# A gated hybrid block on one core: the opening's loads in written order, and side loads placed by unit

## The chip, the core and the metric

The kernel runs on one core of one Trainium2 chip. The metric is the time of one execution on the device, in microseconds (us). Times are taken as the median of several runs; one further execution is recorded by the hardware profiler, and its profile and trace are what is read here.

## What is computed

One sub-layer for a sequence of 1024 rows of width 2048, everything in float32:

```python
mod = c_act @ w_ada + b_ada                       # 3 x 2048
shift, scale, gate = split(mod, 3)
h = rms_norm(x, g_pre) * (1 + scale) + shift      # 1024 x 2048
q_a, f_a, i_a, z_a, gate_bb, gate_cc, v_b, z_b = split(h @ w_in, 8)   # w_in 2048 x 8192
y_a = rms_norm(hgrn2_chunkwise(q_a, log_f, k_a, i_a), g_head_a) * silu(z_a)
y_b = gate_bb * conv3(gate_cc * v_b) * silu(z_b)
m_a, m_b = split(sigmoid(h @ w_merge + b_merge), 2)                   # w_merge 2048 x 4096
out = (m_a * (y_a @ w_up_a) + m_b * (y_b @ w_up_b)) @ w_o
return x + gate * rms_norm(out, g_post)
```

## The kernel before

Each large product is a two by two block product done with seven products in place of eight (Strassen's way; the stages are called p1, p6, p2, p7, p5, p4, p3), on sums and differences of the blocks. To keep float32's precision, each operand is split into a high part in a rounded format (`w_hi`) and the rest (`w_lo`), and each product is three matmuls: high by high, high by low, low by high. `mm3` (L118) issues them, L119, L122 and L123 being the three. `split_w` (L126) makes a weight tile's high part on ScalarE and its low part on VectorE (L131); `split_h` (L134) does it for the other operand, its low part on VectorE at L136.

**Opening.** `load_x` (L177) loads x as 16 tiles of 512 KB, `norm_x` scales the rows, `transpose_x` turns them with TensorE into 16 tiles `xT`, copied out of PSUM by VectorE and ScalarE in turn (L209 to 212). `ada_pair(q)`, for q = 0 to 3, makes a quarter of scale and shift from 16 tiles of w_ada (`ada_load`, L218, 512 KB each): the scale row with one-row matmuls on TensorE (`prow`, L235), the shift row with sums on VectorE (`row_v`, L237 and L239). Small matmuls then turn both rows into columns. `factors_a` applies them to `xT` and makes the operands of the first four stages, `fp1`, `fp6`, `fp2` and `fp7`, of a pair of groups g; eight groups in all. The tiles of x, xT, w_ada and the factors share 38 buffers of 512 KB (tag "big"); every third w_ada tile goes into one of four buffers of its own (tag "ada").

**Units.** `unit_a(u)` (L328) runs 48 times, 32 units for w_in and 16 for w_merge. `load_q` (L323) loads a unit's four 512 KB weight tiles `a11`, `a21`, `a22`, `a12` into five buffers (tag "raw"). VectorE makes the sums s1 and s2 (L338, L339), s4 (L350) and a11 - a21 (L354), and TensorE the products p1, p6, p2 and p7 with the splits of a11, s2, a12 and a11 - a21, 24 matmuls each, into the PSUM tiles `px` and `py`. s1, s4 and the results go to DRAM for the second phase.

**Side work.** The loop over units (L400) also writes, for the units up to 14 that are even, `factors_b(u // 2)` (L287; four sums, L292 to L295, three splits and three stores), which prepares operands for the second phase; for units 16 to 31 two `gate_step`s each (L362), one w_ada tile's load (L365) and two VectorE sums, every eighth followed by a small matmul `pg` (L377); and for the even units from 32 on `sums_o` (L388), four w_o loads and four sums.

**Second phase and after.** The products p5, p4 and p3 of every unit (tile `pz` first), with the recurrence and the convolution beside them; then the two `up` passes, the output projection and the end.

**What sets the order.** The kernel writes instructions unit by unit; the framework's scheduler then orders each engine's queue by its own estimate of times, within the dependences. SP issues all loads in the order of its queue. An instruction given to `keep_in_program_order` keeps its place among the others so given; an instruction written within `issue_after(i)` comes after i.

Of the kernel before, what the change touches and what calls it, by code (L numbers as in the profile page):

```python
# [983 lines left out]
```

## Time and profile before

| | |
|---|---|
| Median of 3 runs | 2768.53 us (2767.21 to 2771.9) |
| The profiled execution's own time | 2769.2 us |
| Its span | 2767.5 us |
| TensorE busy | 2673.0 us, 97% |
| VectorE, ScalarE, GpSimd busy | 62%, 33%, 10% |
| Mean granted TensorE clock | 0.984 of full |

The span goes from the first to the last instruction of the profiled execution; the time adds what lies around it. Busy shares are means over stages that differ. A granted clock of 1.00 is 2.4 GHz, TensorE's upper level; 0.50 would be 1.2 GHz, the lower one.

### The profile page before, as it was taken

To read this page: it belongs to the slowest core of one execution; us is meant where nothing else is said; L and a number is where in the kernel's file an instruction comes from. 1 tells how busy PE (TensorE), PEld (TensorE's weight loads), DVE (VectorE), ACT (ScalarE), POOL (GpSimd) and SP (SyncE) were. 2 spreads that over 40 slices of the span, in tenths; PEclk is the share of its full clock that TensorE was granted. 3 is DMA by queue.
4 is the path that set the end of the run, shared out by engine and by line. 5 is a ranking of instruction groups with operands and counts; after the bars stand their busy time and mean duration, and the time that the engine had idled before them with its cause. 6 is when DMAs were issued, how large, how long until landed. Compare 5 with 4: busy or idle time off the path is not lost.

```text
span 2767.5 us, 31307 instructions
## 1 busy us (share of the span) xinstructions
PE 2673.0 (97%) x11851; PEld 2152.7 (78%) x11851; DVE 1716.7 (62%) x2096; ACT 906.3 (33%) x1176; POOL 280.0 (10%) x495
## 2 busy tenths in 40 slices
PE   4889999999999999999999999999998999999997
PEld 3267878888888888888888888888885787888786
DVE  6777886754554444546666666656563666765667
ACT  4433222222222222233344444435442222232333
POOL 2012111110000000010000000002111101100000
PEclk9899999999999999999999999999998999999999
DMA  9769999985556655584444444359999569773353
GB/s 361 286 201 313 345 349 364 346 292 179 179 192 179 182 175 177 174 316 137 133 130 133 138 146 138 110 178 374 360 363 407 187 213 335 235 282 99 99 178 142
DMA packets 420071, 631.30 MB, mean 228 GB/s; under 512 B 19564, under 2 KB 281808, under 8 KB 419792
## 3 DMA queue, kind: packets, MB, share of 16 engines
q1 hardware_dynamic: 358528, 394.31, 44.7%
q0 software_dynamic: 60208, 230.78, 21.7%
q10 hardware_dynamic: 1184, 4.20, 0.4%
q8 instruction: 93, 1.52, 0.2%
q14 instruction: 58, 0.48, 0.0%
HBM read 431.04 MB, written 198.18 MB: 227 GB/s over the span
## 4 chain that ended last, share of the span: by engine, by line
PE 81%; issue 8%; DMA 7%; DVE 2%; POOL 1%; ACT 1%; DVEq 0%; POOLq 0%; ACTq 0%; SPq 0%
PE po L866 10%; PE pz L119 7%; PE pz L122 7%; PE pz L123 7%; PE px L119 6%; PE px L123 6%; PE px L122 6%; PE py L123 6%; PE py L119 6%; PE py L122 6%; PE pw L119 4%; PE pw L122 4%; PE pw L123 4%; DMA yp<-yf_scr 3%; DMA ga_raw<-in_w_ada_dram 2%
## 5 line engine op out<-in xcount | busy, mean ns | idle before, releaser
L130 ACT CAST w_hi<-w_raw 128x1024 fp32r<-128x1024 f32 (+1 forms) x296 | 290.9, 983 | 1001.6 <-PE px L122 402.5
L131 DVE TENSOR_TENSOR w_lo<-w_raw,w_hi 128x1024 fp32r<-128x1024 f32 (+1 forms) x296 | 335.7, 1134 | 273.1 <-ACT w_hi L130 263.4
L123 PE MATMUL py<-fp,w_lo 128*128 128x512 f32 x768 | 301.2, 392 | 6.9 <-DVE w_lo L131 6.9
L123 PE MATMUL px<-fp,w_lo 128*128 128x512 f32 x768 | 300.9, 392 | 5.2 <-DVE w_lo L131 5.2
L119 PE MATMUL px<-fp,w_hi 128*128 128x512 f32 x768 | 301.2, 392 | 0.0
L122 PE MATMUL py<-fp,w_hi 128*128 128x512 f32 x768 | 299.5, 390 | 1.3 <-DVE fp L136 1.3
L119 PE MATMUL py<-fp,w_hi 128*128 128x512 f32 x768 | 299.8, 390 | 0.9 <-ACT w_hi L130 0.9
L122 PE MATMUL px<-fp,w_hi 128*128 128x512 f32 x768 | 300.0, 391 | 0.0
L866 PE MATMUL po<-w_hi,lt 128*128 128x512 f32 x896 | 244.2, 390 | 0.6 <-DVE og L900 0.6
L866 PEld LDWEIGHTS po<-w_hi,lt 128*128 128x128 f32 x896 | 168.1, 188 | 37.2 <-DVE og L900 2.2
L130 ACT CAST w_hi<-s 128x512 fp32r<-128x512 f32 (+1 forms) x112 | 90.1, 805 | 285.9 <-PE py L122 245.5
L123 PEld LDWEIGHTS py<-fp,w_lo 128*128 128x128 f32 x768 | 144.5, 188 | 41.5 <-DVE w_lo L131 11.2
L123 PEld LDWEIGHTS px<-fp,w_lo 128*128 128x128 f32 x768 | 144.8, 188 | 36.9 <-DVE w_lo L131 6.5
L122 PEld LDWEIGHTS py<-fp,w_hi 128*128 128x128 f32 x768 | 144.5, 188 | 32.1 <-DVE fp L136 1.7
L122 PEld LDWEIGHTS px<-fp,w_hi 128*128 128x128 f32 x768 | 145.1, 189 | 30.8 <-issue 0.5
L119 PEld LDWEIGHTS px<-fp,w_hi 128*128 128x128 f32 x768 | 144.9, 189 | 30.8 <-issue 0.7
L119 PEld LDWEIGHTS py<-fp,w_hi 128*128 128x128 f32 x768 | 144.5, 188 | 30.8 <-ACT w_hi L130 1.3
L119 PE MATMUL pz<-fp,hi 128*128 128x512 f32 x384 | 152.5, 397 | 3.0 <-DVE d L701 3.0
L122 PE MATMUL pw<-fp,w_hi 128*128 128x512 f32 x384 | 150.8, 393 | 0.0
L119 PE MATMUL pz<-fp,w_hi 128*128 128x512 f32 x384 | 150.5, 392 | 0.0
L123 PE MATMUL pz<-fp,lo 128*128 128x512 f32 x384 | 150.4, 392 | 0.0
L119 PE MATMUL pw<-fp,w_hi 128*128 128x512 f32 x384 | 150.4, 392 | 0.0
(286 smaller groups left out, 4959.4 us busy)
## 6 DMA issues: line engine op xcount, KB each, us to landing
w_raw<-in_w_in_dram SPq DMA_DIRECT2D x160, 512.0 KB, 5.2
s_scr<-s POOLq DMA_DIRECT2D x96, 512.0 KB, 6.0
s_raw<-s_scr SPq DMA_DIRECT2D x96, 512.0 KB, 4.3
w_raw<-in_w_merge_dram SPq DMA_DIRECT2D x80, 512.0 KB, 5.7
u_scr<-o POOLq DMA_DIRECT2D x48, 768.0 KB, 7.5
ada_raw<-in_w_ada_dram SPq DMA_DIRECT2D x64, 512.0 KB, 10.8
yf_scr<-yp POOLq DMA_DIRECT2D x56, 512.0 KB, 9.0
yp<-yf_scr SPq DMA_DIRECT2D x56, 512.0 KB, 12.8
```

The source lines that it names most:

```text
L119: mm = nc.tensor.matmul(o, ah, bh, start=first, stop=False, skip_group_check=True)
L122: nc.tensor.matmul(o, ah, bl, start=False, stop=False, skip_group_check=True)
L123: nc.tensor.matmul(o, al, bh, start=False, stop=last, skip_group_check=True)
L130: nc.scalar.copy(out=hi, in_=raw)
L131: nc.vector.tensor_sub(out=lo, in0=raw, in1=hi.bitcast(F32))
L866: nc.tensor.matmul(o, a, b[:, c], start=st, stop=sp, skip_group_check=True)
```

## The change

1. Loads of x, of w_ada, of unit 0's and 1's weights, and the gate's and w_o's, go through `load`, which keeps them in written order.
2. Unit 0's loads, its sums and three of its weight splits are written ahead of `ada_pair(3)` (`unit_a` is now a generator, stopped at `yield`); its products p1, p6 and p2 are pinned in the order groups 0 to 5 of each, then 6 and 7 of each, with p2 in a PSUM tile of its own. All the rest of unit 0 is issued after the last factor of `factors_a`.
3. From unit 2 on, a11 has one buffer of its own; the other three tiles share the five.
4. `factors_b` is written behind units 2, 4, ..., 16 and issued after that unit's last sum. The gate loads are written at units 10 to 25, two a unit, the w_o loads at the even units 26 to 40; their sums are issued after the last sum of the unit that follows.
5. Buffers: the three small row tables share one raw buffer; `row_p` lies in unit 0's result tile `o0`; only the last quarter of w_ada uses a set of its own, every fourth tile, two buffers in place of four.
6. In the second half of `transpose_x`, four of the eight copies on VectorE go to ScalarE.

```diff
-    rows_c = const.tile([16, P], F32, name="rows_c")
+    rows = wp.tile([P, S], F32, tag="raw", name="rows", bufs=5)
+    rows_a, rows_b, rows_c = rows[0:80, 0:P], rows[0:49, P:2 * P], rows[0:16, 2 * P:3 * P]
...
+    def load(o, i):
+        tc.keep_in_program_order(nc.sync.dma_start(out=o, in_=i))
...
+    o0 = ph.tile([P, 3, HS], F32, name="o0", bufs=1)
...
-            nc.sync.dma_start(out=t, in_=x[si * P:(si + 1) * P, q * S:(q + 1) * S])
+            load(t, x[si * P:(si + 1) * P, q * S:(q + 1) * S])
...
-            if k % 2:
+            if k % 2 and (hf == 0 or k % 4 == 1):
                 nc.vector.tensor_copy(out=xT[k][:, halves[hf]], in_=p)
...
-        if n_ada[0] % 3:
+        if q < 3 or n_ada[0] % 4:
             raw = bigt(F32, "ada_raw").rearrange("p (k e) -> p k e", k=2)
         else:
-            raw = ph.tile([P, 2, HS], F32, tag="ada", name="ada_raw", bufs=4)
-        nc.sync.dma_start(out=raw, in_=w_ada_v[:, k:k + 2, t, q * HS:(q + 1) * HS])
+            raw = ph.tile([P, 2, HS], F32, tag="ada", name="ada_raw", bufs=2)
+        load(raw, w_ada_v[:, k:k + 2, t, q * HS:(q + 1) * HS])
...
-        row_p, row_v = (ph.tile([P, HS], F32, tag=t, name=t) for t in ("row_p", "row_v"))
+        row_p, row_v = o0[:, 0], ph.tile([P, HS], F32, tag="row_v", name="row_v")
...
+    def load_a(u):
+        view, e1, e2 = units[u]
+        if u > 1:
+            a11 = ph.tile([P, 8, P], F32, tag="a11", name="a11")
+            nc.sync.dma_start(out=a11, in_=view[:, 0, :, e1:e1 + P])
+        else:
+            a11 = load_q(view, 0, e1, pin=True)
+        return [a11] + [load_q(view, *a, pin=u < 2) for a in ((0, e2), (1, e2), (1, e1))]
...
+    def unit_a(u, raws):
+        a11, a21, a22, a12 = raws
+        o = ph.tile([P, 3, HS], F32, tag="o", name="o", bufs=2) if u else o0
...
+        s4 = ph.tile([P, 8, P], F32, tag="s4", name="s4") if u else s1
...
         if u == 0:
-            for gs in (range(6), (6, 7)):
-                product(px, w1, fa["p1"], pin=True, gs=gs)
-                product(py, w6, fa["p6"], pin=True, gs=gs)
+            v.tensor_sub(out=a21, in0=a11, in1=a21)
+            w2 = split_w(a12, out_t=(ph.tile([P, 8, P], F32R, name="hi3a", bufs=1), wp.tile([P, 8, P], F32R, tag="raw", name="lo3a", bufs=5)))
+            yield
+            p2 = ps("mm", "p2")
+            for gs in (range(6), (6, 7)):
+                for p, w, f in ((px, w1, "p1"), (py, w6, "p6"), (p2, w2, "p2")):
+                    product(p, w, fa[f], pin=True, gs=gs)
...
-        product(px, split_w(a12), fa["p2"], more=True)
-        nc.scalar.copy(out=o[:, 0], in_=px)
-        nc.vector.tensor_sub(out=a21, in0=a11, in1=a21)
+        if u:
+            product(px, split_w(a12), fa["p2"], more=True)
+            nc.scalar.copy(out=o[:, 0], in_=px)
+        else:
+            v.tensor_add(out=o[:, 0], in0=o[:, 2], in1=p2)
+        if u:
+            v.tensor_sub(out=a21, in0=a11, in1=a21)
         product(py, split_w(a21), fa["p7"], more=True)
-        nc.vector.tensor_add(out=o[:, 2], in0=o[:, 2], in1=py)
+        last_sum[0] = v.tensor_add(out=o[:, 2], in0=o[:, 2], in1=py).ins
...
     for q in range(1, 4):
+        if q == 3:
+            first = unit_a(0, load_a(0))
+            next(first)
         ada_pair(q)
         factors_a((2 * q - 2, 2 * q - 1))
-    factors_a((6, 7), vec=(7,))
+    with tc.issue_after(factors_a((6, 7), vec=(7,)).ins):
+        next(first, None)
...
     def gate_step(n):
...
-        nc.sync.dma_start(out=raw, in_=w_ada_v[:, 2 * kq:2 * kq + 2, 2, eb * HS:(eb + 1) * HS])
+        load(raw, w_ada_v[:, 2 * kq:2 * kq + 2, 2, eb * HS:(eb + 1) * HS])
+        yield
...
     def sums_o(g):
...
-            nc.sync.dma_start(out=t, in_=w_o_v[:, par, g, :, c, :])
+            load(t, w_o_v[:, par, g, :, c, :])
+        yield
...
+    side = []
     for u in range(NU):
-        unit_a(u)
-        if u < 16:
-            if u % 2 == 0:
-                factors_b(u // 2)
-        elif u < 32:
-            gate_step(2 * u - 32)
-            gate_step(2 * u - 31)
-        elif u % 2 == 0:
-            sums_o((u - 32) // 2)
+        if u:
+            for _ in unit_a(u, load_a(u)):
+                pass
+
+        with tc.issue_after(last_sum[0]):
+            if u in range(2, 18, 2):
+                factors_b(u // 2 - 1)
+            for f in side:
+                next(f, None)
+        side = []
+        if 10 <= u < 26:
+            side = [gate_step(2 * u - 20), gate_step(2 * u - 19)]
+        elif u in range(26, 42, 2):
+            side = [sums_o((u - 26) // 2)]
+        for f in side:
+            next(f)
```

In the three places that follow, a name's number is its tile's, and tiles are numbered in the order in which they are written.

SP's queue from the last tile of x on; `w_raw` are weight tiles of the units, `ga_raw` the gate's. Before:

```order
L180 DMA x_1_429<-in_x_dram 128x1024
L224 DMA ada_raw<-in_w_ada_dram 128x2x512 x4
L325 DMA w_raw<-in_w_in_dram 128x8x128 x5
L224 DMA ada_raw<-in_w_ada_dram 128x2x512 x60
L325 DMA w_raw<-in_w_in_dram 128x8x128 x21
L365 DMA ga_raw<-in_w_ada_dram 128x2x512
L325 DMA w_raw<-in_w_in_dram 128x8x128
L365 DMA ga_raw<-in_w_ada_dram 128x2x512 x4
```

Now:

```order
L119 DMA x_1_428<-in_x_dram 128x1024
L119 DMA ada_raw<-in_w_ada_dram 128x2x512 x48
L119 DMA w_raw<-in_w_in_dram 128x8x128 x4
L119 DMA ada_raw<-in_w_ada_dram 128x2x512 x16
L119 DMA w_raw<-in_w_in_dram 128x8x128 x4
L318 DMA a_1443<-in_w_in_dram 128x8x128
L311 DMA w_raw<-in_w_in_dram 128x8x128 x7
```

Before, four w_ada tiles and five weight tiles follow x, then the other 60 w_ada tiles, with the weights of the first six units and the gate's first loads behind them. Now 48 w_ada tiles follow x, then unit 0's four weight tiles, the last 16 of w_ada and unit 1's four. Within the 64 w_ada tiles the numbers jump before (the first four are 722, 732, 746 and 756, the 60 begin 714, 716, 724, 730); now they rise in pairs, a scale and a shift tile, as `ada_pair` reads them.

VectorE where unit 0's weight sums stand. Before, between the factors of the last groups (`a_c`, `sh_c`: the columns of scale and shift):

```order
L338 TENSOR_TENSOR s1_1184<-w_raw_1177,w_raw_1179 128x1024
L248 SCALAR_TENSOR_TENSOR a_c_397<-a_c_397,cols_386 128x4
L339 TENSOR_TENSOR s2_1185<-s1_1184,w_raw_1175 128x1024
L354 TENSOR_TENSOR w_raw_1177<-w_raw_1175,w_raw_1177 128x1024
L266 TENSOR_SCALAR xT_14_570<-xT_14_570,a_c_397,sh_c_398 128x1024
L266 TENSOR_SCALAR keep3_1136<-xT_15_577,a_c_397,sh_c_398 128x512
L266 TENSOR_SCALAR xT_15_577<-xT_15_577,a_c_397,sh_c_398 128x512
L350 TENSOR_TENSOR s4_1186<-w_raw_1181,s2_1185 128x1024
L278 TENSOR_TENSOR xT_12_556<-keep3_1136,xT_12_556 128x512
L278 TENSOR_TENSOR xT_14_570<-keep3_1136,xT_14_570 128x512
L131 TENSOR_TENSOR w_lo_1197<-s2_1185,w_hi_1196 128x1024
L136 TENSOR_TENSOR fp1_6_1143<-xT_12_556,fp1_6_1143 128x512
```

Now, between the third and the fourth quarter of the shift row:

```order
L243 SCALAR_TENSOR_TENSOR row_v_904<-ada_raw_963,c_act_379,row_v_904 128x512 x2
L134 TENSOR_TENSOR w_lo_1030<-w_raw_1017,w_hi_1029 128x1024
L251 TENSOR_TENSOR a_c_396<-pa_970,cols_384 128x4
L253 TENSOR_TENSOR sh_c_397<-pa_970,cols_384 128x4
L252 SCALAR_TENSOR_TENSOR a_c_396<-a_c_396,cols_384 128x4
L336 TENSOR_TENSOR s1_1025<-w_raw_1019,w_raw_1021 128x1024
L337 TENSOR_TENSOR s2_1026<-s1_1025,w_raw_1017 128x1024
L341 TENSOR_TENSOR w_raw_1019<-w_raw_1017,w_raw_1019 128x1024
L241 TENSOR_SCALAR row_v_1046<-ada_raw_1049,c_act_379 128x512
L134 TENSOR_TENSOR lo3a_1042<-w_raw_1023,hi3a_1041 128x1024
L243 SCALAR_TENSOR_TENSOR row_v_1046<-ada_raw_1049,c_act_379,row_v_1046 128x512
L134 TENSOR_TENSOR w_lo_1037<-s2_1026,w_hi_1036 128x1024
```

The sums and low parts of unit 0 have moved ahead of the last quarter's sums (`row_v_1046`) and of the factors that hang on it.

VectorE at the first of `factors_b` (the four sums into `xx`). Before, right behind the last factor of the opening:

```order
L131 TENSOR_TENSOR w_lo_1283<-w_raw_1177,w_hi_1282 128x1024
L136 TENSOR_TENSOR fp7_7_1168<-xT_14_570,fp7_7_1168 128x512
L292 TENSOR_TENSOR xx_1312<-fp6_0_886 128x512
L293 TENSOR_TENSOR xx_1312<-fp2_0_894 128x512
L294 TENSOR_TENSOR xx_1312<-xx_1312 128x512
L295 TENSOR_TENSOR xx_1312<-keep0_871,xx_1312 128x512
L131 TENSOR_TENSOR w_lo_1344<-w_raw_1329,w_hi_1343 128x1024
L136 TENSOR_TENSOR fb0_0_1317<-xx_1312,fb0_0_1317 128x512
```

Now, behind unit 2's last sum (`o_1451`), with sums of units 3 and 4 around it:

```order
L360 TENSOR_TENSOR w_raw_1736<-a11_1734,w_raw_1736 128x1024
L362 TENSOR_TENSOR o_1451<-o_1451,py_1456 128x512
L297 TENSOR_TENSOR xx_1580<-fp6_0_883 128x512
L298 TENSOR_TENSOR xx_1580<-fp2_0_891 128x512
L134 TENSOR_TENSOR w_lo_1643<-s2_1607,w_hi_1642 128x1024
L299 TENSOR_TENSOR xx_1580<-xx_1580 128x512
L337 TENSOR_TENSOR s2_1744<-s1_1743,a11_1734 128x1024
L300 TENSOR_TENSOR xx_1580<-keep0_868,xx_1580 128x512
```

Before, all eight of `factors_b` stand within units 0 to 5; now one stands behind every second unit from 2 to 16.

## Rows read from the trace of the kernel before

**Rows 1.** The page, list of engines: busy us (share of the span) xinstructions

```profile
PE 2673.0 (97%) x11851; PEld 2152.7 (78%) x11851; DVE 1716.7 (62%) x2096; ACT 906.3 (33%) x1176; POOL 280.0 (10%) x495
```

**Rows 2.** Windows: us, PE, PEld, DVE, ACT, POOL busy (x), PEclk, DMA share, GB/s

```profile
0.00:20.00 20.00, 3.73 (x14) 2.54 (x14) 10.49 (x27) 11.53 (x19) 10.29 (x17) 1.00 0.91 336
20.00:40.00 20.00, 14.24 (x81) 12.33 (x82) 15.38 (x36) 15.39 (x27) 6.26 (x5) 0.92 1.11 347
40.00:60.00 20.00, 16.50 (x66) 6.27 (x64) 16.23 (x23) 3.17 (x6) 0.00 (x0) 1.00 1.05 387
60.00:80.00 20.00, 7.20 (x21) 3.94 (x22) 4.24 (x6) 0.57 (x1) 0.00 (x0) 0.52 0.89 325
80.00:100.00 20.00, 19.34 (x51) 5.24 (x51) 16.40 (x28) 10.10 (x15) 0.00 (x0) 0.84 0.55 184
100.00:120.00 20.00, 17.65 (x45) 4.12 (x43) 16.62 (x29) 10.10 (x15) 0.00 (x0) 0.87 1.04 383
```

**Rows 3.** Timeline, TensorE: start us, us, engine line op, xcount [idle before]

```profile
136.10 3.38 PE L235 MATMUL prow<-ada_raw,c_act 128*1 128x512 f32 x4 [2.75 <-DMA ada_raw<-in_w_ada_dram]
...
142.04 0.48 PE L119 MATMUL px<-fp,w_hi 128*128 128x512 f32 x1
...
143.01 0.63 PE L119 MATMUL px<-fp,w_hi 128*128 128x512 f32 x1
...
143.44 0.63 PE L122 MATMUL px<-fp,w_hi 128*128 128x512 f32 x1
...
168.79 0.39 PE L119 MATMUL py<-fp,w_hi 128*128 128x512 f32 x1
...
174.23 0.39 PE L119 MATMUL px<-fp,w_hi 128*128 128x512 f32 x1
```

**Rows 4.** Timeline, VectorE, the opening

```profile
73.49 0.48 DVE L237 TENSOR_SCALAR row_v<-ada_raw,c_act 128x512 f32<-128x512 f32 x1 [15.80 <-DMA ada_raw<-in_w_ada_dram]
...
98.08 0.49 DVE L237 TENSOR_SCALAR row_v<-ada_raw,c_act 128x512 f32<-128x512 f32 x1 [3.32 <-DMA ada_raw<-in_w_ada_dram]
...
103.72 1.54 DVE L239 SCALAR_TENSOR_TENSOR row_v<-ada_raw,c_act,row_v 128x512 f32<-128x512 f32 x2 [2.71 <-DMA ada_raw<-in_w_ada_dram]
...
135.11 4.68 DVE L239 SCALAR_TENSOR_TENSOR row_v<-ada_raw,c_act,row_v 128x512 f32<-128x512 f32 x6
...
142.36 1.21 DVE L338 TENSOR_TENSOR s<-w_raw 128x1024 f32<-128x1024 f32 x1
```

**Rows 5.** Waits of TensorE, 142 to 175 us: us, times, longest

```profile
PE py L123 <- DVE w_lo L131: 2.7, 1, 2.7
PE px L123 <- DVE w_lo L131: 2.2, 1, 2.2
PE py L122 <- DVE fp L136: 1.3, 1, 1.3
```

**Rows 6.** Tiles pz and pg: ns min/median/max, first and last start us

```profile
L119 PE MATMUL pz<-fp,w_hi x384: 389/389/499, 1213.6 to 2086.9; 128*128 128x512 f32 x192
...
L377 PE MATMUL pg<-gacc,ones x8: 591/592/592, 301.0 to 393.6; 128*128 128x512 f32 x8
```

**Rows 7.** Windows, units 1 to 47, columns as in rows 2

```profile
200.00:280.00 80.00, 75.46 (x324) 61.37 (x323) 64.54 (x80) 28.08 (x39) 15.58 (x30) 0.98 0.90 314
...
600.00:900.00 300.00, 300.00 (x1325) 248.09 (x1324) 151.33 (x140) 70.94 (x82) 22.93 (x43) 1.00 0.59 184
...
sum 1039.40, PE 1031.25 PEld 848.18 DVE 617.67 ACT 256.19 POOL 121.96; mean PE 171.88 PEld 141.36 DVE 102.94 ACT 42.70 POOL 20.33
```

**Rows 8.** Factors_b's first sum, gate loads, SP's waits, landing of weights

```profile
L292 DVE TENSOR_TENSOR xx<-fp x8: 679/686/693, 164.8 to 253.1; 128x512 f32<-128x512 f32 x8
...
L365 SPq DMA_DIRECT2D ga_raw<-in_w_ada_dram x32: 367/394/4886, 263.4 to 377.4; - x32
...
SPq L365 <- DVE gacc L374: 25.3, 19, 3.2
...
w_raw<-in_w_in_dram SPq DMA_DIRECT2D x160, 512.0 KB, 5.2
```

More of the change, by code (lines that the diff above doesn't have):

```diff
@@ L75, in tile_hgrn2_shortconv_block @@
     make_identity(nc, ident)
-    rows_c = const.tile([16, P], F32, name="rows_c")
+    rows = wp.tile([P, S], F32, tag="raw", name="rows", bufs=5)
+    rows_a, rows_b, rows_c = rows[0:80, 0:P], rows[0:49, P:2 * P], rows[0:16, 2 * P:3 * P]
     nc.scalar.dma_start(out=rows_c, in_=c[0].rearrange("(n p) -> n p", p=P))
-    rows_a = const.tile([80, P], F32, name="rows_a")
-    rows_b = const.tile([49, P], F32, name="rows_b")
     b_rows = b_ada[0].rearrange("(n p) -> n p", p=P)
@@ L135, in split_h @@
         eng(out=t[:, 0], in_=raw)
-        nc.vector.tensor_sub(out=t[:, 1], in0=raw, in1=t[:, 0].bitcast(F32))
+        return nc.vector.tensor_sub(out=t[:, 1], in0=raw, in1=t[:, 0].bitcast(F32))
     STAGES = ("p1", "p6", "p2", "p7", "p5", "p4", "p3")
@@ L272, in keep_f @@
             fa[s][g] = pair(f"f{s}_{g}")
-            split_h(fa[s][g], raw, nc.scalar.copy)
+            return split_h(fa[s][g], raw, nc.scalar.copy)
         for g, b11, b12, b21, b22 in parts:
@@ L283, in factors_a @@
         for g, b11, b12, b21, b22 in parts:
-            keep_f("p7", g, b12)
+            last = keep_f("p7", g, b12)
+        return last
     def factors_b(g):
@@ L299, in factors_b, with load_q @@
             nc.gpsimd.dma_start(out=hb_scr[n][g], in_=t.rearrange("p a b -> p (a b)").bitcast(F32))
+    units = [(w_in_v, (2 * j) * 1024 + i * P, (2 * j + 1) * 1024 + i * P) for i in range(NH) for j in range(4)]
+    units += [(w_merge_v, 256 * m, 256 * m + P) for m in range(16)]
+    def load_q(view, par, e0, pin=False):
+        raw = wp.tile([P, 8, P], F32, tag="raw", name="w_raw", bufs=5)
+        (load if pin else nc.sync.dma_start)(raw, view[:, par, :, e0:e0 + P])
+        return raw
+    def load_a(u):
[6 more added lines that the diff above has]
+        return [a11] + [load_q(view, *a, pin=u < 2) for a in ((0, e2), (1, e2), (1, e1))]
@@ new lines, in tile_hgrn2_shortconv_block @@
+    last_sum = [None]
+    def unit_a(u, raws):
+        a11, a21, a22, a12 = raws
+        o = ph.tile([P, 3, HS], F32, tag="o", name="o", bufs=2) if u else o0
+        s1, s2 = (ph.tile([P, 8, P], F32, tag=f"s{n}", name=f"s{n}", bufs=1) for n in (1, 2))
+        s4 = ph.tile([P, 8, P], F32, tag="s4", name="s4") if u else s1
+        px, py = ps("mm", "px"), ps("mm", "py")
+        v = nc.vector
+        w1 = split_w(a11)
+        if u:
+            product(px, w1, fa["p1"])
+        v.tensor_add(out=s1, in0=a21, in1=a22)
+        v.tensor_sub(out=s2, in0=s1, in1=a11)
+        nc.gpsimd.dma_start(out=s_scr[u][:, 0], in_=s1.rearrange("p a b -> p (a b)"))
+        w6 = split_w(s2)
+        if u == 0:
+            v.tensor_sub(out=a21, in0=a11, in1=a21)
[5 more added lines that the diff above has]
+                    product(p, w, fa[f], pin=True, gs=gs)
+        nc.scalar.copy(out=o[:, 2], in_=px)
+        if u:
+            product(py, w6, fa["p6"])
+        v.tensor_add(out=o[:, 1], in0=o[:, 2], in1=py)
+        v.tensor_sub(out=s4, in0=a12, in1=s2)
+        nc.gpsimd.dma_start(out=s_scr[u][:, 1], in_=s4.rearrange("p a b -> p (a b)"))
+        if u:
[3 more added lines that the diff above has]
+            v.tensor_add(out=o[:, 0], in0=o[:, 2], in1=p2)
+        if u:
+            v.tensor_sub(out=a21, in0=a11, in1=a21)
+        product(py, split_w(a21), fa["p7"], more=True)
+        last_sum[0] = v.tensor_add(out=o[:, 2], in0=o[:, 2], in1=py).ins
+        nc.gpsimd.dma_start(out=u_scr[u], in_=o)
```

30 lines of the change are left out of this document (1 added, 29 removed).

## The prediction

> **What bounds the kernel now.** I read the page's list of engines first: TensorE is busy for 97% of the span [rows 1]. So time can only come from stretches in which TensorE has nothing to do, or does something other than the big products. The windows over the opening show where that is [rows 2]: until 120 us TensorE's work is transposes and one-row products, and the DMA moves 336 to 387 GB/s while it is fed, but only 184 between 80 and 100. The timeline of TensorE dates the rest [rows 3]: the last tile of w_ada is waited for until 136.10, the first product of unit 0 starts at 142.04, unit 1 at 174.23. Unit 1's stretch ends with the first product of the second phase, at 1213.6 [rows 6].
>
> The timeline of VectorE shows what the opening waits for [rows 4]. It stands still for 15.80 us until 73.49, because the scheduler has put four later w_ada tiles and five weight tiles ahead of the tiles that are summed next; two more waits for w_ada tiles, 3.32 and 2.71 us, follow. The change has three places: this opening, unit 0, and units 1 to 47.
>
> **The opening.** Two limits hold it, and I take the later one.
>
> Transfers: ahead of the last w_ada tile now stand 16 tiles of x, 64 of w_ada and 4 of unit 0, 84 of 0.524 MB, 44.0 MB, and the first store of unit 0's sums, 0.5 more. In the first 40 us x and the first tiles came at 336 and 347 GB/s, 13.7 MB [rows 2]; nothing there changes. 30.9 MB are left. At 347 GB/s they take 89 us, at 387 (the best stretch) 80; I take the mean of the three stretches that ran unhindered, 347, 387 and 383, so 372 and 83 us: the last tile lands at 123, between 120 and 129. From the last tile of the before to the first product 5.9 us passed (136.10 to 142.04), 3.4 of them four one-row products; now two VectorE sums (0.8 each, from six in 4.68 [rows 4]) and the small products that turn the row into columns (1.05 and half that of hand-over) follow, about 3 us: 126. The Trainium skill's page "DMA: Bandwidth & Descriptors" (Specifications) gives a core about 358 GB/s of HBM, less than this trace shows in two stretches; by that figure the last tile lands at 126.3 and the whole comes out near 2741.
>
> VectorE: its last sum ended at 139.8 (135.11 + 4.68). The 15.8 us wait goes, and the two tile waits of 6.0 us too; for that it gets unit 0's sums and low parts ahead of the last w_ada sums: three sums, three low parts, 1.2 us each (the 1.21 of [rows 4]), 7.2 us. 139.8 - 15.8 - 6.0 + 7.2 = 125.2, and with the 2.25 us that passed before between the last sum and the first product (139.8 to 142.04) it is 127.5. Moving four of the second half's copies of x to ScalarE is taken at nothing: ScalarE is free there. Merging rows_a, rows_b and rows_c into a weight buffer, and row_p into o0, saves space alone; the copies wait for the one-row product of their own quarter, long after the last reader.
>
> So the first product starts at 127.5 instead of 142.04: **14.5 us**, between 7 (129 and the old 5.9) and 19.5 (120 and 2.5).
>
> **Unit 0.** It took 174.23 - 142.04 = 32.2 us; the same 96 matmuls at the pace of its last product (24 in 5.44 us, 168.79 to 174.23 [rows 3]) are 21.76. Of the 10.4 us between, 6.1 are three waits [rows 5], for low parts and for a factor whose sums stood behind unit 0's and unit 1's weight sums on VectorE. The other 4.3 are matmuls at the lower clock: 143.01 to 143.44 is 0.43 us for one, the pace of 1.2 GHz, where 0.227 is the pace later, at 2.4. After the change the weights of three products are split before the last quarter of w_ada, and 54 matmuls instead of 36 run on factors that are ready, 12.2 us in place of 8.2. In that time VectorE makes the last two groups' factors without any weight sum between (15 instructions, most of half width, 0.7 us each, 11 us, the earliest needed first), so I count all three waits as gone. Between 60 and 80, around TensorE's long wait, the granted clock was 0.52 [rows 2]; the opening keeps smaller gaps, so half of the 4.3 stays. What is late next is unit 1: its first low part now stands on VectorE behind unit 0's last sum, which waits for unit 0's last matmul. 0.8 + 1.2 less the two matmuls that need no low part (0.45) is 1.5 us of new wait, and its sums queue behind that, perhaps 0.5 more. Together: -6.1 - 2.1 + 2 = **-6 us**, between 0 and -8.4.
>
> **Units 1 to 47.** From 174.23 to 1213.6 are 1039.4 us; 47 units of 21.76 are 1022.7, and the gate's eight matmuls at 0.59 [rows 6] are 4.7. So 12.0 us are lost. TensorE's idle time is 8.15 of it (1039.40 less 1031.25 in the sum of [rows 7]), and between 600 and 900 it is zero. What is different before 600 is the crowd: all eight factors_b stand between 164.8 and 253.1 us and all 32 gate loads between 263.4 and 377.4 [rows 8], with the DMA at 314 GB/s and VectorE 81% busy from 200 to 280 [rows 7], where 600 to 900 has 184 GB/s and 50%. The change puts factors_b behind the sums of every second unit from 2 to 16, and the gate loads into units 10 to 25, two a unit: 1 MB more in 21.8 us, 48 GB/s over the 184. So these units become like those from 600 to 900. Factors_b adds seven half-width instructions, 5 us, to every second unit's VectorE time of 11 (50% of 21.8); that fits. I leave 3 us for what is not seen: **-9 us**, between -12 and 0.
>
> The weight tile of its own costs no instruction. Three of a unit's four tiles now share five buffers where four did, so these come earlier; the fourth can only be loaded once the unit before has split its own, at about that unit's start, 21 us ahead of need against 5.2 us of landing [rows 8]. Everything from the second phase on keeps its order but for a swap or two in the upward products; zero, within 2 us.
>
> **Sum.** The profiled execution took 2769.2 us against the median of 2768.5, so both serve. 2769.2 - 14.5 - 6 - 9 = 2739.7; less the 0.7 between the two, **2739 us**. A measurement here tells about 0.2% (5.5 us) from nothing.
>
> **Rivals.**
> *VectorE paces the opening (0.20).* Only the long wait goes, the short ones are for work of its own: 139.8 - 15.8 + 7.2, the product at 133.4, a gain of 8.6. For it speaks that VectorE is busy 16.4 and 16.6 of 20 us at 80 to 120 [rows 2]; against it, that the two short waits name w_ada tiles. 2769 - 8.6 - 6 - 9 = 2745.
> *The units keep their losses (0.13).* The waits between 174 and 600 come from weight tiles landing late for other reasons, and move. For it: at the start unit 1's and unit 2's tiles still come after the opening. Against: from 600 to 900 there are none, with the same tiles. 2769 - 14.5 - 6 = 2748; with the first rival 2754.
> *Slower: SP's queue becomes the wait (0.06).* SP issues in order; the side loads are now fixed among the weight loads, and where one waits for a free wide buffer, which factors_b's stores, a gate sum or an output sum must release, the weights behind it wait too, and VectorE's sums run a unit ahead and stand in front of the low parts. The gate loads did wait there, 25.3 us in 19 waits, 3.2 the longest [rows 8]. If TensorE then loses its longest wait of unit 0, 2.7 us [rows 5], in each of the 24 units that carry side loads, it is 65 us: 2804. It decides from 29.5 / 24 = 1.2 us a unit on. The same page of the Trainium skill (Anatomy of one DMA) says that a semaphore wait is taken on the issuing sequencer, before dispatch; by it nothing behind such a load could pass, and SP's 19 waits agree. Against it: before, 32 of these loads stood in a third of the time, and TensorE lost 8 us.
> *It does little (0.04).* The opening is bound by some limit these views don't show and the units likewise: 2766.
>
> **Chances.** My forecast has 0.57. Faster by over 0.2%: the forecast and the first two rivals, 0.90; within 0.2%: 0.04; slower: 0.06. The range takes in the fast ends of the three terms in part (19.5 + 8.4 + 12 would be 2729) and the first two rivals together: 2728 to 2757.
>
> **What would show it.** Right: VectorE's 15.8 us wait gone and the DMA at 345 GB/s or more from 20 to 115 us; the first product at 124 to 130; unit 1 some 24 us behind it; no wait of TensorE over 1 us between unit 2 and the second phase, which starts near 1184. Wrong in the opening: a first product at 133 or later with VectorE busy to the end. Wrong in the units: waits for low parts at the units with side loads, with a gate or output load as what VectorE's sums wait for.

## The result, and the profile after

The changed kernel takes 2896.5 us in the median of 4 runs (2890.7 to 2904.4) against 2768.3 before: a ratio of 1.0469, interval 1.0446 to 1.0492. It is 128 us slower; the forecast was 2739.

The page's span and list of engines, against [rows 1]; here, as in every fence below, of the changed kernel unless another is named:

```profile
span 2889.0 us, 31267 instructions
...
PE 2713.8 (94%) x11851; PEld 2168.9 (75%) x11851; DVE 1708.0 (59%) x2093; ACT 907.8 (31%) x1179; POOL 279.8 (10%) x495
```

TensorE's work is the same 11851 matmuls, but its busy time has grown by 41 us and its idle time by 81: matmuls have become slower too, for the most part since the clock falls after waits (below). The lines of the changed kernel's code stand a few further down: L122, L125 and L126 are the three matmuls of `mm3`, L134 makes a weight's low part, L336 is s1, L337 is s2, L360 is a11 - a21, L318 the load of a11 into its own buffer (tile `a`), L311 that of the other weights, L119 a load kept in order. Three stretches tell where the time went.

**The opening gained about what was expected.** Windows over it, columns as in [rows 2]:

```profile
20.00:40.00 20.00, 15.27 (x74) 10.79 (x75) 15.66 (x36) 14.47 (x26) 6.42 (x5) 0.83 1.04 392
...
80.00:100.00 20.00, 15.91 (x44) 4.37 (x44) 18.27 (x31) 11.05 (x16) 0.00 (x0) 0.91 1.10 353
100.00:120.00 20.00, 14.30 (x33) 3.76 (x34) 18.08 (x26) 8.52 (x11) 0.60 (x1) 0.83 0.99 362
```

VectorE's long wait of [rows 4] is gone, and the DMA moves 353 to 392 GB/s throughout. TensorE's timeline, as in [rows 3]:

```profile
122.43 1.88 PE L239 MATMUL prow<-ada_raw,c_act 128*1 128x512 f32 x4 [0.89 <-DMA ada_raw<-in_w_ada_dram]
...
130.37 1.87 PE L248 MATMUL pa<-ones,row_v 128*128 128x1 f32 x8 [4.35 <-DVE row_v L243]
132.10 0.78 PE L122 MATMUL px<-fp,w_hi 128*128 128x512 f32 x1
...
157.12 0.39 PE L122 MATMUL px<-fp,w_hi 128*128 128x512 f32 x1
```

TensorE's last tile of w_ada is there at 122.4; VectorE's, the last of all, landed at 124.4 by the trace (136.1 before). The first product starts at 132.1 (142.0), unit 1 at 157.1 (174.2). Between the last tile and the first product stand VectorE's sums, for which TensorE waits 4.35 us; timeline of VectorE:

```profile
98.02 4.68 DVE L243 SCALAR_TENSOR_TENSOR row_v<-ada_raw,c_act,row_v 128x512 f32<-128x512 f32 x6
...
125.64 4.68 DVE L243 SCALAR_TENSOR_TENSOR row_v<-ada_raw,c_act,row_v 128x512 f32<-128x512 f32 x6
```

The last six begin at 125.6, after their tiles have landed, and end at 130.3. So in this trace VectorE, not the transfers, is what the first product waits for last.

**The units lost 140 us.** The second phase's first product, of the list of tile `pz` (ns min/median/max, first and last start in us), answers to [rows 6]:

```profile
L122 PE MATMUL pz<-fp,w_hi x384: 388/389/500, 1336.0 to 2209.2; 128*128 128x512 f32 x192
```

Units 1 to 47 took 1336.0 - 157.1 = 1178.9 us, where they took 1039.4 before. From there to the end of the span it is 1553.0 us now and 1553.9 before: nothing. The sum is -17.1 + 139.5 - 0.9 = 121.5, the difference of the two spans.

In the page's groups the loss stands in one operation, the matmul with a low part, and one line of VectorE has a large wait before it (busy, mean ns, idle before and what ended it):

```profile
L126 PE MATMUL py<-fp,w_lo 128*128 128x512 f32 x768 | 309.6, 403 | 51.5 <-DVE w_lo L134 51.4
...
L360 DVE TENSOR_TENSOR w_raw<-a,w_raw 128x1024 f32<-128x1024 f32 x46 | 56.3, 1223 | 188.2 <-DMA a<-in_w_in_dram 127.9
```

The waits between 157 and 1336 us (us, times, longest), of TensorE first, to compare with [rows 5], then of VectorE:

```profile
PE py L126 <- DVE w_lo L134: 51.4, 31, 5.9
PE px L126 <- DVE w_lo L134: 42.1, 18, 5.2
```

```profile
DVE w_raw L360 <- DMA a<-in_w_in_dram: 127.9, 23, 8.6
DVE s L337 <- DMA a<-in_w_merge_dram: 67.4, 7, 10.1
DVE s L336 <- DMA w_raw<-in_w_in_dram: 63.1, 20, 7.0
DVE w_raw L360 <- DMA a<-in_w_merge_dram: 60.3, 9, 8.5
DVE s L336 <- DMA w_raw<-in_w_merge_dram: 59.2, 11, 9.6
...
DVE s L337 <- DMA a<-in_w_in_dram: 19.2, 4, 9.0
```

TensorE waits for low parts, 94 us in 49 waits; VectorE, which makes them, waits 275 us for the load of a11, in the two lines that read it first (L360 and L337), and 122 us for the other weights. One such place, from the timelines of VectorE, SP and TensorE:

```profile
807.82 1.22 DVE L134 TENSOR_TENSOR w_lo<-a,w_hi 128x1024 fp32r<-128x1024 f32 x1
811.83 0.69 DVE L362 TENSOR_TENSOR o<-o,py 128x512 f32<-128x512 f32 x1 [2.80 <-PE py L126]
812.44 1.22 DVE L423 TENSOR_TENSOR wo<-wo 128x1024 f32<-128x1024 f32 x1
821.13 1.23 DVE L360 TENSOR_TENSOR w_raw<-a,w_raw 128x1024 f32<-128x1024 f32 x1 [7.47 <-DMA a<-in_w_in_dram]
822.27 1.22 DVE L134 TENSOR_TENSOR w_lo<-s,w_hi 128x1024 fp32r<-128x1024 f32 x1
```

```profile
809.11 0.98 SPq L318 DMA_DIRECT2D a<-in_w_in_dram  x1
```

```profile
817.30 0.39 PE L125 MATMUL py<-fp,w_hi 128*128 128x512 f32 x1
823.55 0.79 PE L126 MATMUL py<-fp,w_lo 128*128 128x512 f32 x1 [5.86 <-DVE w_lo L134]
824.14 0.63 PE L122 MATMUL py<-fp,w_hi 128*128 128x512 f32 x1
824.57 0.63 PE L125 MATMUL py<-fp,w_hi 128*128 128x512 f32 x1
...
827.55 0.41 PE L126 MATMUL py<-fp,w_lo 128*128 128x512 f32 x1
827.80 0.39 PE L122 MATMUL py<-fp,w_hi 128*128 128x512 f32 x1
828.03 0.39 PE L125 MATMUL py<-fp,w_hi 128*128 128x512 f32 x1
```

VectorE makes the low part of a11 at 807.82, the last read of the one buffer; SP issues the next unit's a11 at 809.11, as soon as that is over. The next unit's a11 - a21 (L360) stands behind two short instructions in VectorE's queue and waits for this load until 821.13. Behind it stands the low part of s2 (822.27), which the unit in hand needs: TensorE stops for 5.86 us in the middle of it. Then nine matmuls come 0.43 us apart, the pace of 1.2 GHz, before it is 0.23 again, that of 2.4. In sum over the units:

```profile
157.12:1336.00 1178.88, 1079.59 (x4522) 867.19 (x4521) 618.41 (x631) 257.08 (x307) 123.34 (x231) 0.97 0.69 220
```

The idle time there is 99.3 us. The busy time of 1079.6 is 56.9 more than 47 times 21.76, of which the gate's matmuls are 4.7. Of the other 52, some 30 are matmuls at the lower clock (about 145 in the trace start 0.38 us or more before the next one), and most of the rest stands at the two ends of the waits: the last matmul before one counts with its whole 0.39 us, where others start 0.227 apart, and the first after it takes longer too.

### The profile page after: what moved, and what is told of

The parts are those of the page before. It is cut to its first block, busy times and chain, and to the rows that moved or that the text cites. A ratio compares the mean times of both kernels' runs of the same rounds, so it can differ in the third digit from the quotient of the medians.

```text
span 2889.0 us, 31267 instructions
## 1 busy us (share of the span) xinstructions
PE 2713.8 (94%) x11851; PEld 2168.9 (75%) x11851; DVE 1708.0 (59%) x2093; ACT 907.8 (31%) x1179; POOL 279.8 (10%) x495
## 4 chain that ended last, share of the span: by engine, by line
PE 53%; DMA 6%; DVE 2%; issue 1%; ACT 0%; DVEq 0%; SPq 0%; ACTq 0%
PE po L904 9%; PE pz L122 7%; PE pz L126 7%; PE pz L125 7%; PE pw L122 3%; PE pw L125 3%; PE pw L126 3%; DMA yp<-yf_scr 3%; DMA a<-in_w_merge_dram 2%; PE px L126 2%; PE px L122 2%; PE px L125 2%; PE py L126 2%; PE py L122 2%; PE py L125 2%; PE sc L590 1%
## 5 line engine op out<-in xcount | busy, mean ns | idle before, releaser
L133 ACT CAST w_hi<-w_raw 128x1024 fp32r<-128x1024 f32 (+1 forms) x249 | 241.1, 968 | 860.1 <-PE py L125 238.9
L134 DVE TENSOR_TENSOR w_lo<-w_raw,w_hi 128x1024 fp32r<-128x1024 f32 (+1 forms) x249 | 278.0, 1116 | 136.3 <-ACT w_hi L133 134.0
L126 PE MATMUL py<-fp,w_lo 128*128 128x512 f32 x768 | 309.6, 403 | 51.5 <-DVE w_lo L134 51.4
L126 PE MATMUL px<-fp,w_lo 128*128 128x512 f32 x760 | 309.5, 407 | 42.3 <-DVE w_lo L134 42.1
L122 PE MATMUL py<-fp,w_hi 128*128 128x512 f32 x768 | 305.9, 398 | 5.5 <-DVE o L351 4.6
L125 PE MATMUL py<-fp,w_hi 128*128 128x512 f32 x768 | 304.8, 397 | 0.0
L122 PE MATMUL px<-fp,w_hi 128*128 128x512 f32 x760 | 304.1, 400 | 0.0
L125 PE MATMUL px<-fp,w_hi 128*128 128x512 f32 x760 | 304.0, 400 | 0.0
L126 PEld LDWEIGHTS py<-fp,w_lo 128*128 128x128 f32 x768 | 147.8, 192 | 97.6 <-DVE w_lo L134 67.2
L126 PEld LDWEIGHTS px<-fp,w_lo 128*128 128x128 f32 x760 | 147.9, 195 | 84.7 <-DVE w_lo L134 53.0
L122 PEld LDWEIGHTS py<-fp,w_hi 128*128 128x128 f32 x768 | 147.9, 193 | 37.8 <-issue 6.0
L125 PEld LDWEIGHTS py<-fp,w_hi 128*128 128x128 f32 x768 | 147.9, 193 | 31.9
L125 PEld LDWEIGHTS px<-fp,w_hi 128*128 128x128 f32 x760 | 147.5, 194 | 32.3 <-issue 0.2
L122 PEld LDWEIGHTS px<-fp,w_hi 128*128 128x128 f32 x760 | 148.3, 195 | 31.0 <-issue 0.5
L360 DVE TENSOR_TENSOR w_raw<-a,w_raw 128x1024 f32<-128x1024 f32 x46 | 56.3, 1223 | 188.2 <-DMA a<-in_w_in_dram 127.9
L122 PE MATMUL pz<-fp,hi 128*128 128x512 f32 x384 | 152.7, 398 | 3.0 <-DVE d L739 3.0
L125 PE MATMUL pw<-fp,w_hi 128*128 128x512 f32 x384 | 150.9, 393 | 0.0
L336 DVE TENSOR_TENSOR s<-w_raw 128x1024 f32<-128x1024 f32 x48 | 58.7, 1224 | 155.3 <-DMA w_raw<-in_w_in_dram 63.1
L122 PE MATMUL pw<-fp,w_hi 128*128 128x512 f32 x384 | 150.4, 392 | 0.0
```

The lines of the kernel that those rows point to most:

```text
L122: mm = nc.tensor.matmul(o, ah, bh, start=first, stop=False, skip_group_check=True)
L125: nc.tensor.matmul(o, ah, bl, start=False, stop=False, skip_group_check=True)
L126: nc.tensor.matmul(o, al, bh, start=False, stop=last, skip_group_check=True)
L133: nc.scalar.copy(out=hi, in_=raw)
L134: nc.vector.tensor_sub(out=lo, in0=raw, in1=hi.bitcast(F32))
L336: v.tensor_add(out=s1, in0=a21, in1=a22)
```

## The experiments

Theory A is that VectorE's queue holds the first read of the next a11, whose single buffer came free only at the read just before, ahead of this unit's low parts. Rivals: the side loads, now fixed in SP's queue, hold the weights back (B), or both are needed (C). The table has the median, the ratio to the kernel before, run beside it (2765.8 to 2766.4 us in the experiments), with its interval, and from each trace the start (us) of unit 1's and of the second phase's first product and what is lost per stretch of units (us; time less 21.76 a unit, the eight gate matmuls of 0.59 included).

| kernel | median | ratio | unit 1 | phase 2 | 1-9 | 10-25 | 26-41 | 42-47 |
|---|---|---|---|---|---|---|---|---|
| before | 2768.3 | | 174.2 | 1213.6 | 12.3 | 2.7 | 1.2 | 0.5 |
| changed | 2896.5 | 1.0469 (1.0446-1.0492) | 157.1 | 1336.0 | 16.2 | 42.0 | 79.0 | 18.9 |
| e1 a11 shared | 2771.8 | 1.0018 (1.0009-1.0028) | 157.0 | 1210.1 | 5.1 | 10.9 | 11.6 | 2.7 |
| e2 before, a11 own | 2832.9 | 1.0242 (1.0227-1.0257) | 169.6 | 1275.0 | 13.6 | 11.1 | 43.3 | 14.7 |
| e3 side work as before | 2834.3 | 1.0249 (1.0232-1.0266) | 165.7 | 1283.5 | 25.5 | 10.1 | 44.0 | 15.5 |
| e4 read later | 2757.5 | 0.9968 (0.9956-0.9979) | 159.0 | 1202.6 | 2.1 | 11.6 | 5.6 | 1.5 |
| e5 opening only | 2761.4 | 0.9987 (0.9976-0.9999) | 161.5 | 1205.2 | 16.3 | 2.2 | 1.7 | 0.8 |
| e6 shared and later | 2762.8 | 0.9987 (0.9977-0.9996) | 157.2 | 1205.3 | 2.1 | 11.6 | 9.6 | 2.2 |
| e7 later, unpinned | 2759.6 | 0.9977 (0.9965-0.9990) | 156.4 | 1199.0 | 2.1 | 12.0 | 5.7 | 0.0 |
| e8 two buffers | 2757.0 | 0.9963 (0.9950-0.9976) | 156.7 | 1195.6 | 2.2 | 8.2 | 4.3 | 1.5 |
| e9 factors_b placed only | 2761.8 | 0.9985 (0.9976-0.9994) | 158.0 | 1210.5 | 5.8 | 21.6 | 1.8 | 0.5 |
| e10 e9 with two buffers | 2764.7 | 0.9996 (0.9987-1.0005) | 158.1 | 1205.9 | 2.1 | 22.6 | 0.0 | 0.3 |
| e11 unit 0 on GpSimd | 2761.8 | 0.9984 (0.9975-0.9993) | 161.9 | 1203.6 | 2.1 | 8.4 | 6.3 | 2.1 |
| e12 later, w_o free | 2756.6 | 0.9964 (0.9950-0.9978) | 155.5 | 1194.4 | 2.1 | 9.3 | 4.7 | 0.0 |

### One buffer for a11: taken away, put in alone, left alone

e1, on the changed kernel:

```diff
-        if u > 1:
-            a11 = ph.tile([P, 8, P], F32, tag="a11", name="a11")
-            nc.sync.dma_start(out=a11, in_=view[:, 0, :, e1:e1 + P])
-        else:
-            a11 = load_q(view, 0, e1, pin=True)
+        a11 = load_q(view, 0, e1, pin=u < 2)
```

> The changed kernel with one edit: a11 loaded into the five shared weight buffers in every unit, as the other three tiles. Theory A (VectorE's queue holds the next unit's first read of a11, whose single buffer came free only one load earlier, ahead of this unit's low parts): the waits for low parts in units 10 to 47 vanish, unit 1 starts at 157 as in the changed kernel, the second phase at about 1189, time 2740 to 2752. Theory B (the side loads, now fixed among the weight loads in SP's queue, hold back the weights behind them): little changes, 2860 to 2900. Theory C (both are needed: the load of a11 lands late only where side loads share the DMA): 2740 to 2752, as A.

125 of the 128 us come back, so B falls. But A's 2740 to 2752 was missed too: the units still lose 30 us, more than before, and the median is 0.2% above the kernel before. Of these, 25 lie in units 10 to 47, where the gate's and w_o's work is placed; with all side work left free (e5) units 10 to 47 lose 4.7.

e2 puts the same buffer into the kernel before, from unit 2 on, and changes nothing else (the removed lines of e1's diff, without the pin).

> The kernel before with one edit: from unit 2 on a11 has one buffer of its own, the other three tiles share the five. A: TensorE loses 2 to 3 us in each of 46 units by waits for low parts, as the changed kernel does in its units without side loads, less the 12 us that the kernel before lost there already: 2850 to 2895, slower than before by 80 to 125. B: no change, 2768. C: a loss only where the gate loads and w_o loads stand, 2775 to 2805.

The buffer alone costs 67 us, with no side load placed: between A and C. The cleanest place is in units without any side work. Timelines of VectorE, SP and TensorE, of e2:

```profile
1026.25 1.22 DVE L131 TENSOR_TENSOR w_lo<-a,w_hi 128x1024 fp32r<-128x1024 f32 x1
1035.55 1.22 DVE L359 TENSOR_TENSOR w_raw<-a,w_raw 128x1024 f32<-128x1024 f32 x1 [8.09 <-DMA a<-in_w_merge_dram]
1036.69 0.68 DVE L361 TENSOR_TENSOR o<-o,py 128x512 f32<-128x512 f32 x1
1037.29 1.22 DVE L131 TENSOR_TENSOR w_lo<-s,w_hi 128x1024 fp32r<-128x1024 f32 x1
```

```profile
1027.49 0.37 SPq L332 DMA_DIRECT2D a<-in_w_merge_dram  x1
```

```profile
1038.56 0.50 PE L123 MATMUL py<-fp,w_lo 128*128 128x512 f32 x1 [1.01 <-DVE w_lo L131]
```

SP issues the load 0.02 us after the last read of a11 (1026.25 + 1.22) has ended; VectorE's next instruction waits 8.09 us for it, a whole round of a transfer, and the low part of s2 follows two instructions behind. Inside e2 the order also shows why A's number was too high: in units 15 to 17 the scheduler has put no low part of the unit behind the next a11's first read, in 18 to 20 none or the last one only, and units 15 to 20 lose nothing; from unit 22 on three low parts stand behind it, and from unit 24 on every unit but the last two loses 1.7 us or more (units 22 and 23 lose nothing yet).

e3 writes the side work of the changed kernel as before, without `issue_after` and pins, and keeps the buffer:

> The changed kernel with the side work (factors_b, gate, w_o sums) written and left to the scheduler as in the kernel before; a11 keeps its own buffer. A: 17 us gained up to unit 1, then 2 to 3 us lost in each of 46 units: 2845 to 2885. B: the loss of the units goes, 2745 to 2755. C: 2760 to 2800.

Between A and C again, and from unit 10 on the units lose per stretch what they lose in e2. Against the changed kernel (79 us in units 26 to 41) it is 44: side loads nearly double the loss where they share the DMA with a11. In the place shown above a11 took 12 us from issue to its read. By the trace's landing times the changed kernel's a11 of units 28 to 41 takes 10 to 12 us beside w_o's loads and 5.5 to 7 us without them, where e3 has 7 to 9 throughout. SP issues it each time within 1.1 us of the last read, so its queue (B) isn't what holds this load back. And unit 1 starts at 165.7, not 157, and units 1 to 9 lose 25.5 us: much of the opening's gain went with the side work; e5 takes that up.

### The order alone, and the time of the load alone

e4 keeps one buffer and every side load, and moves two VectorE instructions:

```diff
-        v.tensor_sub(out=s2, in0=s1, in1=a11)
+        if u > 1:
+            with tc.issue_after(lo3[0]):
+                v.tensor_sub(out=s2, in0=s1, in1=a11)
+                v.tensor_sub(out=a21, in0=a11, in1=a21)
...
+            w2 = split_w(a12)
+            lo3[0] = last_lo[0]
```

> The changed kernel, all buffers and side loads kept; only VectorE's order is edited: from unit 2 on the two first reads of the next unit's a11 (s2 and a11 - a21) are issued after this unit's third low part. A: a11 has then 8 us and more to land before it is read, the waits for low parts go for the most part, 2740 to 2765. B: no gain, 2880 to 2900. C: part of the loss stays where the w_o loads stand, 2770 to 2830.

139 us come back. TensorE's waits for low parts in units 1 to 47, of e4:

```profile
PE px L126 <- DVE w_lo L136: 4.3, 5, 2.1
PE py L126 <- DVE w_lo L136: 4.0, 5, 1.5
```

From 94 us to 8.3, with the same buffers and transfers: A's order is shown to be the loss.

e8 leaves the order and starts the load earlier: `bufs=2` for a11, and 4 instead of 5 wherever the tag "raw" is used.

> The changed kernel with two buffers for a11 and four instead of five for the other three tiles (and for what else uses that set), so the same memory; VectorE's first read of the next a11 still stands ahead of the low parts. A: the load of a11 now starts a unit earlier, so the read finds it there; the second phase starts at 1195 to 1225 and the time is 2750 to 2780 (later phases have one buffer fewer). If it is the order or the number of the other three tiles' buffers that counts: the second phase at 1310 or later, 2870 to 2920.

As A said, and against the answer that only the order counts. The first read still stands ahead of the low parts, but the load was issued a unit before, timelines of SP and VectorE, of e8:

```profile
753.66 0.41 SPq L318 DMA_DIRECT2D a<-in_w_in_dram  x1
```

```profile
777.52 1.23 DVE L336 TENSOR_TENSOR s<-w_raw 128x1024 f32<-128x1024 f32 x1 [3.39 <-DMA w_raw<-in_w_in_dram]
778.78 1.23 DVE L360 TENSOR_TENSOR w_raw<-a,w_raw 128x1024 f32<-128x1024 f32 x1
...
780.52 1.22 DVE L134 TENSOR_TENSOR w_lo<-s,w_hi 128x1024 fp32r<-128x1024 f32 x1
```

Issued at 753.66 and read at 778.78, 25 us later, without a wait; units 1 to 47 as a whole:

```profile
156.70:1195.60 1038.90, 1029.90 (x4522) 847.39 (x4521) 625.10 (x631) 256.53 (x307) 123.34 (x231) 1.00 0.78 250
```

Idle 9.0 us instead of 99.3, and the busy time 49.7 us less: the slower matmuls were the waits' second price. The Trainium skill's page "Trainium Kernel Development and Optimization" (Best Practices) asks to double-buffer so that transfers overlap work; here that is 139 us against a single buffer (though e8 also takes one from the other three tiles), and e4 gives as much without it.

e6 is e1 with e4's order.

> The changed kernel with a11 in the shared buffers and, besides, s2 and a11 - a21 of the next unit issued after this unit's third low part. If VectorE's order alone was the loss (A): the 16 us of low-part waits that were left with shared buffers go too, 2745 to 2758, as with the buffer of its own and the later read. If the buffer of its own earns something once the order is right: 2762 to 2772.

2762.8, at the lower edge of the second answer: some 5 us above e4, but the two intervals still touch. That the buffer of its own earns something once the order is right is likely, not shown.

### The side work

e5 is e1 with the side work as before:

> The changed kernel with a11 in the shared buffers and all side work as in the kernel before: of the change only the opening and unit 0 are left. Theory D (the scheduler pulls factors_b, when it is left free, into units 0 and 1, and that eats what the opening gains): first product at 132 to 134, but unit 1 at 170 to 176, time 2760 to 2772. Rival (the opening's gain stands by itself): unit 1 at 157, units as before, time 2745 to 2753.

Theory D holds in time (2761.4) and, as the lines below show, in cause; unit 1, at 161.5, lies between the two answers. In e5 the first product starts at 131.3, and VectorE and ScalarE then show factors_b's four sums (`xx`) and splits (`fb`) in unit 0, timelines of VectorE, ScalarE and TensorE:

```profile
157.05 0.69 DVE L297 TENSOR_TENSOR xx<-fp 128x512 f32<-128x512 f32 x1
...
159.11 0.69 DVE L300 TENSOR_TENSOR xx<-keep,xx 128x512 f32<-128x512 f32 x1
```

```profile
159.88 0.62 ACT L138 CAST fb<-xx 128x512 fp32r<-128x512 f32 x1 [7.37 <-DVE xx L300]
160.40 1.04 ACT L133 CAST w_hi<-w_raw 128x1024 fp32r<-128x1024 f32 x1
```

```profile
161.49 0.79 PE L122 MATMUL px<-fp,w_hi 128*128 128x512 f32 x1 [5.17 <-ACT w_hi L133]
```

Unit 1's high part stands behind a split of factors_b on ScalarE, which waits for its sums on VectorE, and TensorE waits 5.17 us for it. Of the 17 us that the changed kernel gains up to unit 1, 12.7 are left here, and units 1 to 9 then lose 16.3 us. e9 differs from e5 in the place of factors_b alone: unit 1 starts at 158.0, units 1 to 9 lose 5.8, and unit 10 starts 14 us earlier than in e5. So placing factors_b behind units 2 to 16 lets the opening's gain through as far as unit 10. The medians show nothing of it (2761.8 and 2761.4), because e9 loses it again in units 10 to 25, as follows.

e7 is e4 with `nc.sync.dma_start` for the gate's and w_o's loads in place of `load`:

> The kernel of the later read, with the gate's and w_o's loads given back to the scheduler's order; their sums stay where the change puts them. If the waits that were left there (units 16 to 18, 41 and 43) come from side loads fixed ahead of weight loads in SP's queue (B, small): 2743 to 2752. If not: 2755 to 2775, the loads crowding into earlier units.

2759.6 lies in the second answer and 2 us above e4: that pins in SP's queue cost anything is not shown.

e9 is e1 with the gate's and w_o's work as before; e10 the same on e8.

> The changed kernel with a11 in the shared buffers; factors_b stays placed behind units 2 to 16, but the gate's and w_o's loads and sums are written where the kernel before has them and left to the scheduler. If placing factors_b is what the opening needs, and the gate and w_o loads placed by unit are what costs the units 10 to 47 their 25 us with shared buffers: unit 1 at 157, units 1 to 47 lose 11 to 17 as before, the second phase at 1191 to 1197, time 2744 to 2753. If the gate and w_o loads do no harm where the change puts them: no better than with shared buffers alone, 2762 to 2775.

> The last one, but with two buffers for a11 and four for the other three tiles. If the side loads were the rest of the loss with two buffers (units 15 to 47: some 8 us), 2745 to 2752; if not, 2755 to 2765. Since the first read of a11 stands ahead of the low parts in its units 1 to 28 again, it also tests the two buffers a second time: no unit there should lose over 2 us.

e9's time, 2761.8, lies between its answers; e10's, 2764.7, in its second, but its units 18, 22 and 24 lost 4.4 to 7.5 us where none should have lost over 2. So leaving the side loads free does not win back the rest of the loss. Left free, the gate's loads crowd: SP's rows of the tile `ga_raw` in e10 and, placed by the change, in e8 (x32, ns, first and last start):

```profile
L393 SPq DMA_DIRECT2D ga_raw<-in_w_ada_dram x32: 367/376/4887, 508.4 to 627.9; - x32
```

```profile
L119 SPq DMA_DIRECT2D ga_raw<-in_w_ada_dram x32: 367/368/2213, 386.2 to 692.7; - x32
```

In 120 us instead of 306, and units 10 to 25 lose 22.6 us instead of 8.2. So spreading the gate over the units was right here, by up to 14 us. Why it was is open: the crowd alone isn't the reason, since in e5 and in the kernel before the same 32 loads stand in 114 us (235 to 349 and [rows 8]), and e5's units 4 to 9 lose 5.9 us, gate matmuls included. w_o's loads look the other way: left free, units 26 to 47 lose 0.3 us (e10), placed 5.8 (e8). But e10's w_o loads start at 634 us, in unit 23, so part of the 22.6 may be theirs. No unit of e10 outside 18 to 24 lost over 2 us but unit 1, at 2.1.

e12 takes the better of each: e4 with w_o's work as before.

> The kernel of the later read with a11 in its own buffer, factors_b and the gate's loads placed as the change has them, and only w_o's loads and sums written where the kernel before has them and left to the scheduler, which draws them into units 26 to 37. If w_o's loads placed by unit were the 6 us that units 26 to 47 still lost there: these units lose under 2 us, the second phase at 1195 to 1199, time 2749 to 2755, the best of the study. If a crowd of w_o loads costs as the crowd of gate loads did: 2757 to 2770.

Here the second phase starts at 1194.4, the earliest of all, and the profiled span, 2747.6, is the shortest; the median, 2756.6, is 1.6 above what was expected and no different from e4's and e8's; units 26 to 47 lose 4.7 us, not under 2. These three beat the kernel before, by 0.3 to 0.4%. That w_o's loads are better left free is not shown.

### What paces the opening

e11 is e8 with unit 0's s1 and a11 - a21 on `nc.gpsimd`:

> The kernel with two buffers for a11, with two of unit 0's three weight sums (s1 and a11 - a21) on GpSimd instead of VectorE, 2.4 us less on VectorE ahead of the last quarter's sums. If VectorE paces the opening: first product 2 us earlier than there, at 129 to 130.2. If the transfers pace it: unchanged, 131.3 to 132.3. Time 2753 to 2760 either way.

Missed in place and time: the first product came 5.8 us later than in e8 (131.6), and later than in any other kernel with this opening (130.5 to 134.0). Timelines of TensorE, GpSimd and VectorE of e11:

```profile
137.35 0.77 PE L122 MATMUL px<-fp,w_hi 128*128 128x512 f32 x1
```

```profile
98.88 2.63 POOL L336 TENSOR_TENSOR s<-w_raw 128x1024 f32<-128x1024 f32 x1 [62.61 <-DMA w_raw<-in_w_in_dram]
...
102.46 2.59 POOL L341 TENSOR_TENSOR w_raw<-w_raw 128x1024 f32<-128x1024 f32 x1
```

```profile
99.24 8.72 DVE L243 SCALAR_TENSOR_TENSOR row_v<-ada_raw,c_act,row_v 128x512 f32<-128x512 f32 x6
```

While GpSimd's two sums ran, VectorE's six sums took 8.72 us, where the same six take 4.68 in the changed kernel (98.02). So VectorE got more work instead of less, and the first product followed it. Not all of the 5.8 us is GpSimd's: 1.7 were there before its first sum (in e8 the six sums start at 97.50). That fits VectorE as the one that paces the opening, but the test did not take work from it as meant, so it isn't shown.

## Why the prediction was wrong

- **Opening, -14.5 forecast, -9.9 measured.** The transfers came as worked out (last tile at 124.4 for 123). The VectorE sum failed: 127.5 for 132.1. Both short waits were counted as gain; the first rival, which kept them, said 133.4, and the trace has TensorE waiting for VectorE at the end, as that rival had it. Inside the bounds.
- **Unit 0, -6 forecast, -7.2 measured** (25.0 us for 32.2). Right in size, but for the most part by something that was costed at nothing here: in e5, with factors_b left free, it is 30.2 us to unit 1's first product, so 5.2 of the 7.2 come from keeping factors_b out. The 2 us of new wait came too, but in unit 1, which lost 2.1.
- **Units 1 to 47, -9 forecast, +139.5 measured.** This is the step that failed: "The weight tile of its own costs no instruction", loaded "at about that unit's start, 21 us ahead of need against 5.2 us of landing". The need was dated by TensorE's products. The first to need a11 is VectorE, which reads it for s2 and a11 - a21 up to a unit ahead of the products, as the order showed before anything ran: in the third place of the change, a11 - a21 of unit 4 stands ahead of unit 2's last sum and of unit 3's low part of s2. Between a11's last read and the next a11's first read on VectorE stood no instruction in 25 of 45 places and two in 13, against a round of 6 to 12 us. One buffer made a run-ahead of VectorE, which costs little with shared buffers loaded early (e1), into a wait that everything behind it shares.
- **Also there: the crowd.** That the units with side work would become like those from 600 to 900, with no loss, did not come true even with two buffers: in e8 units 10 to 25 lose 8.2 us, 4.7 of it gate matmuls, and units 26 to 47, with w_o's loads, 5.8. Of the 9 us forecast the units as a whole gained 0.5. The losses before that were blamed on the crowd lay in units 1 to 9 and shrank from 12.3 (some 4 of it gate matmuls, which now stand later) to 2.1 us in e4 and 2.2 in e8: there the reasoning held, for about 6 us.
- **The slower rival (0.06)** had low parts behind sums that run ahead, but put the wait on SP, behind side loads, in 24 units. It came on VectorE, behind a weight load, and in more units (40 of the 47 lost over 0.4 us), with some 3.3 us a unit in the mean in place of 2.7 (156 us of loss in 47, some 30 of it the lower clock).
- **Second phase: zero forecast, -0.9 measured.**

## What to carry to other kernels

A buffer is early enough only if its load is released well ahead of the first read in any engine's queue: follow the order of the engine that runs ahead, and count the instructions between the last read of the old tile and the first read of the new one. Where that is less than a transfer's round (6 to 12 us here), add a second buffer or move the read; either gave back 139 us here. And when an opening is shortened, fix where the scheduler may put work that was waiting for it to end, or that work takes the gap.
